# A two-layer recurrent encoder trunk: the residual kept token-major, output projections with x stationary

## The chip, the cores and the metric

The kernel runs on one core of a Trainium2 chip. A core has five engines that run on their own: TensorE (PE in the profile, with its weight loads as PEld), VectorE (DVE), ScalarE (ACT), GpSimd (POOL) and SyncE (SP), which here only starts transfers. They meet through semaphores. The metric is the device time of one execution in microseconds; lower is better.

## The reference

The input x is 256 tokens by 2048 features, float32. Two layers follow each other; each is a mixer and a gated MLP, each behind an RMSNorm and added to the residual:

```
for layer in range(2):
    hn = rmsnorm(h, norm_mix_g[layer])
    h = h + (mlstm_mixer if layer == 0 else hgrn_mixer)(hn, ...)
    h = h + conv_glu(rmsnorm(h, norm_ffn_g[layer]), ...)
return rmsnorm(h, final_g)
```

`rmsnorm` divides by the root of the mean square over the 2048 features of a token and multiplies by a gain per feature. The mLSTM mixer projects hn to q, k, v, an output gate and 32 gate columns, runs a bidirectional matrix memory over 8 heads, and projects 2048 features back (`w_out`). The HGRN mixer does the like with 16 heads. `conv_glu` projects to 2 x 5504 features, runs a centred convolution of width 3 over the tokens on one half, and projects `gelu(c) * v` back to 2048 (`w_down`).

## The kernel before

Every large product is an exact-enough float32 product made of three fast ones. A weight piece of 1024 columns is fetched as `raw` (SyncE's queue, 1 MB a transfer), rounded on ScalarE to `wh` (L145), and the remainder `wl` is left by a subtraction on VectorE (L146). Activations are held in the same way: a tile `xt` has the rounded value in its first 256 columns and the remainder in the next 256. The product is `wh*xh + wl*xh + wh*xl`.

`stream` walks over a list of chunks, each with a weight source, `nk` inner tiles of 128, and a function `done` that takes the sums out of PSUM. Weight pieces are made three ahead (`LOOK`), with three raw buffers and four of `wh` and `wl`. A chunk has one of these forms:

- "fm", feature-major: the weights are stationary. Two blocks of 128 output features are made; for each inner tile and block, one matmul streams the 512 columns of `xt` (hi and lo at once) and one streams 256 columns against `wl` (L196, L197). The output has features on partitions and tokens along the row.
- "tm", token-major: x is stationary. 512 output features are made for two halves of 128 tokens; for each inner tile and half, three matmuls of 512 columns stream `wh`, `wl`, `wh` (L186 to L188). The output has tokens on partitions.

Queries, keys, decays and the whole up projection are "fm"; values and output gates are "tm". The four kinds of output projection (mLSTM, HGRN, and the two parts of each feed-forward stage, which splits its 43 hidden tiles into 22 and 21) are "fm" chunks of 256 features, eight for each (`project`, L298).

The residual `hx` is feature-major: 16 blocks `hT[k]` of 128 features by 256 tokens. When a projection chunk is done, ScalarE copies the upper half of the sums (`b`, L309) and VectorE adds both halves to the block (L310, L311). `Norm.add` then makes the next stage's `xt` by `split` (L203 on ScalarE, L204 on VectorE) with the gain in it, and GpSimd squares the block and adds it to a running sum (L245, L247). After the last block two matmuls with ones sum the squares over the partitions (L253); `finish` takes the power on GpSimd (L279), spreads the result over the partitions by a diagonal and two matmuls (L285), and copies it out as `R` (L287). Since the factor is per token, `R` is applied to the results of the next stage, not to its inputs.

The last norm's blocks are scaled by their gain into `hg` (L232). The very last chunk is made block by block with 256-column matmuls (L175); at its end the squares are closed, and eight tiles of 512 columns are multiplied by the factor, six on VectorE and two on GpSimd (L787), and stored by eight transfers from two queues (L788).

The recurrences of the heads run beside the projections. They are generators, kept in `Side` and moved on by a count of time that each inner tile adds to (`tick`); `until` and `drain` force them. The program order that comes out is then put through a scheduler that may move instructions within an engine; the hardware runs each engine's list in order.

Of the kernel before, what the change touches and what calls it, by code (L numbers as in the profile page):

```python
# [15 lines left out]
P = 128  # L16
T = 256
# [13 lines left out]
    ("mix_g", 2 * KT), ("ffn_g", 2 * KT), ("a_head_g", KT), ("b_head_g", KT), ("final_g", KT),  # L31
# [21 lines left out]
def trunk_kernel(ctx, tc, xT, pp_d, cst_d, w_first, w_aq, w_ak, w_av, w_ao, w_aout,  # L53
                 w_bq, w_bv, w_bg, w_bout, w_up, w_down, out, mscr, stop=9):
# [15 lines left out]
    hT = [hx[:, k] for k in range(KT)]  # L70
    ident = cst[:, C_ID:C_ID + P]
# [46 lines left out]
    def split_weights(chunks):  # L118

        first = True  # L120
        for ch in chunks:
            total = ch.nk * ch.width
            cuts = [0]
            if ch.last and total % 1024:
                cuts.append(total % 1024)
# [24 lines left out]
    def stream(chunks):  # L150
# [10 lines left out]
        for ch in chunks:  # L161
# [4 lines left out]
            while k < ch.nk:  # L166
                fetch()
                wh, wl, n = ready.pop(0)
                if ch.last:
                    for f in range(2):  # L170
                        for kk in range(n):
                            x, c = ch.x(k + kk), kk * 256 + f * P
                            terms = ((wh, 0), (wl, 0), (wh, T))
                            for i, (w, o) in enumerate(terms):
                                pe.matmul(ps[f][:, 0:T], w[:, c:c + P], x[:, o:o + T], start=(k + kk == 0 and i == 0),  # L175
                                          stop=(k + kk == ch.nk - 1 and i == 2))
                    k += n
                    continue
# [43 lines left out]
    class Norm:  # L222
        def __init__(self, gname, goff, final=False, first=False):
            self.first = first
            self.g, self.o, self.final = gname, goff, final
            self.xs, self.pc = [], None

        def add(self, k):
            if self.final:
                if k % 2 == 0:  # L230
                    self.xs.append(keep.tile([P, 2, T], F32, tag=f"xt{k}", name=f"hg{k}"))
                act.activation(self.xs[k // 2][:, k % 2], hT[k], AF.Copy, scale=col(self.g, self.o + k))  # L232
            else:
                t = keep.tile([P, 2 * T], F32R, tag=f"xt{k}", name=f"xt{k}")
                split(t, hT[k], col(self.g, self.o + k))
                self.xs.append(t)
            if self.first:
                return
# [10 lines left out]
            if k >= (KT - 3 if self.final else KT - 1):  # L249
                if self.pc is None:  # L250
                    self.pc = [aux("pc") for _ in range(2)]
# [621 lines left out]
```

## Time and profile before

| | |
|---|---|
| median of the runs | 2469.77 us (2469.3 to 2469.8, 3 runs) |
| the profiled execution | 2469.78 us, its span 2468.0 us |
| TensorE busy | 2450.2 us, 99% |
| VectorE, ScalarE, GpSimd busy | 1781.9, 1200.8, 272.8 us |
| granted TensorE clock | 0.998 |
| DMA | 449.07 MB, 182 GB/s on average |
| first output projection's first and last matmul | 310.6 and 399.9 us |
| second mixer's output projection | 1646.4 to 1737.1 us |

In rows of groups, the numbers behind the bar are the busy time in us and the mean of one instruction in ns, then the idle time of that engine just before them and what ended it. Matmuls are pipelined: their durations overlap, so the sum of a group's durations is more than the time it takes. The distance between starts in the timeline is what a matmul costs the stream. Rows of the timeline give start (us), duration (us), engine, line, operation and tiles. Rows of stretches give the stretch, its length, then each engine's busy time, then granted clock, DMA share and GB/s. Rows of the chain give start, duration, engine, tile, line.

### The profile page before, as it was taken

To read this page: it belongs to the slowest core of one execution; us is meant where nothing else is said; L and a number is where in the kernel's file an instruction comes from. 1 tells how busy PE (TensorE), PEld (TensorE's weight loads), DVE (VectorE), ACT (ScalarE), POOL (GpSimd) and SP (SyncE) were. 2 spreads that over 40 slices of the span, in tenths; PEclk is the share of its full clock that TensorE was granted. 3 is DMA by queue.
4 is the path that set the end of the run, shared out by engine and by line. 5 is a ranking of instruction groups with operands and counts; after the bars stand their busy time and mean duration, and the time that the engine had idled before them with its cause. 6 is when DMAs were issued, how large, how long until landed. Compare 5 with 4: busy or idle time off the path is not lost.

```text
span 2468.0 us, 35972 instructions
## 1 busy us (share of the span) xinstructions
PE 2450.2 (99%) x13950; PEld 2134.1 (86%) x13950; DVE 1781.9 (72%) x2975; ACT 1200.8 (49%) x1810; POOL 272.8 (11%) x341
## 2 busy tenths in 40 slices
PE   9999999999999999999999999999999999999998
PEld 7888888888888888888888888888888888888887
DVE  7766577777656777678888888887777755677754
ACT  6655455444444445444444444445544444444443
POOL 0100032000000000132222222224000000000022
PEclk9999999999999999999999999999999999999999
DMA  7654555666556555555454544446555555666553
GB/s 260 189 178 167 177 183 188 190 189 191 186 189 199 188 188 189 180 194 178 157 168 154 164 161 156 163 145 202 187 189 188 188 188 190 192 192 193 183 190 124
DMA packets 65915, 449.07 MB, mean 182 GB/s; under 512 B 7616, under 2 KB 8128, under 8 KB 15568
## 3 DMA queue, kind: packets, MB, share of 16 engines
q1 hardware_dynamic: 63936, 443.29, 55.4%
q0 software_dynamic: 800, 2.16, 0.6%
q8 instruction: 109, 1.79, 0.3%
q10 hardware_dynamic: 1008, 1.32, 0.1%
q14 instruction: 62, 0.51, 0.1%
HBM read 444.58 MB, written 2.16 MB: 181 GB/s over the span
## 4 chain that ended last, share of the span: by engine, by line
PE 90%; DVE 7%; issue 1%; ACT 1%; DMA 0%; DVEq 0%; POOL 0%; POOLq 0%
PE mm L196 50%; PE mm L197 25%; PE mm L187 3%; PE mm L188 3%; PE mm L186 3%; DVE wl L146 3%; DVE QK L627 1%; PE pd L626 1%; DVE km L609 1%; PE pn L439 1%; PE mm L175 1%; DVE AT L604 1%; PE py L651 1%; DVE qm L609 1%; DVE G L586 0%
## 5 line engine op out<-in xcount | busy, mean ns | idle before, releaser
L146 DVE TENSOR_TENSOR wl<-raw,wh 128x1024 fp32r<-128x1024 f32 (+1 forms) x864 | 1047.1, 1213 | 553.6 <-ACT wh L145 540.6
L145 ACT CAST wh<-raw 128x1024 fp32r<-128x1024 f32 (+1 forms) x864 | 884.4, 1024 | 895.8 <-PE mm L196 500.4
L196 PE MATMUL mm<-xt,wh 128*128 128x512 f32 x3776 | 1318.5, 395 | 0.0
L197 PE MATMUL mm<-xt,wl 128*128 128x256 f32 x3776 | 1050.8, 278 | 0.0
L196 PEld LDWEIGHTS mm<-xt,wh 128*128 128x128 f32 x3776 | 708.0, 188 | 161.2
L197 PEld LDWEIGHTS mm<-xt,wl 128*128 128x128 f32 x3776 | 709.9, 188 | 0.9
L196 PE MATMUL mm<-g,wh 128*128 128x512 f32 x1334 | 462.6, 394 | 0.0
L197 PE MATMUL mm<-g,wl 128*128 128x256 f32 x1334 | 369.5, 277 | 0.0
L196 PEld LDWEIGHTS mm<-g,wh 128*128 128x128 f32 x1334 | 250.1, 188 | 58.1
L197 PEld LDWEIGHTS mm<-g,wl 128*128 128x128 f32 x1334 | 250.4, 188 | 0.0
L186 PE MATMUL mm<-wh,xt 128*128 128x512 f32 x512 | 203.9, 402 | 2.2 <-ACT xt L203 2.2
L187 PE MATMUL mm<-wl,xt 128*128 128x512 f32 x512 | 204.5, 399 | 0.4 <-DVE wl L146 0.4
L188 PE MATMUL mm<-wh,xt 128*128 128x512 f32 x512 | 201.9, 396 | 0.0
L208 ACT COPY b<-mm 128x256 f32<-128x256 f32 x237 | 87.7, 370 | 178.9 <-PE mm L197 178.9
L242 POOL TENSOR_TENSOR acc<-hx 128x256 f32<-128x256 f32 x4 | 4.8, 1205 | 1239.7 <-DVE hx L311 1239.7
L186 PEld LDWEIGHTS mm<-wh,xt 128*128 128x128 f32 x512 | 96.1, 189 | 21.0 <-ACT xt L203 2.5
L187 PEld LDWEIGHTS mm<-wl,xt 128*128 128x128 f32 x512 | 97.0, 189 | 18.4 <-DVE wl L146 0.8
L188 PEld LDWEIGHTS mm<-wh,xt 128*128 128x128 f32 x512 | 97.0, 189 | 18.4
L196 PE MATMUL mm<-yb,wh 128*128 128x512 f32 x256 | 89.6, 396 | 0.0
L196 PE MATMUL mm<-ya,wh 128*128 128x512 f32 x256 | 89.1, 394 | 0.0
L245 POOL TENSOR_TENSOR sq<-hx 128x256 f32<-128x256 f32 x52 | 62.1, 1202 | 197.8 <-DVE hx L311 195.6
L209 DVE TENSOR_TENSOR a<-mm,b 128x256 f32<-128x256 f32 x86 | 36.5, 424 | 51.0 <-ACT b L208 50.9
(185 smaller groups left out, 2083.2 us busy)
## 6 DMA issues: line engine op xcount, KB each, us to landing
raw<-in_w_up SPq DMA_DIRECT2D x172, 1024.0 KB, 5.2
raw<-in_w_down SPq DMA_DIRECT2D x64, 1024.0 KB, 4.9
raw<-in_w_bq SPq DMA_DIRECT2D x48, 1024.0 KB, 5.1
raw<-in_w_ao SPq DMA_DIRECT2D x16, 1024.0 KB, 4.9
raw<-in_w_aout SPq DMA_DIRECT2D x16, 1024.0 KB, 5.2
raw<-in_w_bv SPq DMA_DIRECT2D x16, 1024.0 KB, 4.9
raw<-in_w_bg SPq DMA_DIRECT2D x16, 1024.0 KB, 4.9
raw<-in_w_bout SPq DMA_DIRECT2D x16, 1024.0 KB, 5.1
```

Of the source, the lines that this page charges most:

```text
L145: act.copy(wh[:, :m], r)
L146: dve.tensor_tensor(wl[:, :m], r, wh[:, :m].bitcast(F32), ALU.subtract)
L175: pe.matmul(ps[f][:, 0:T], w[:, c:c + P], x[:, o:o + T], start=(k + kk == 0 and i == 0), stop=(k + kk == ch.nk - 1 and i == 2))
L186: pe.matmul(ps[t], xh, wh[:, c], start=st, stop=False)
L187: pe.matmul(ps[t], xh, wl[:, c], start=False, stop=False)
L188: pe.matmul(ps[t], xl, wh[:, c], start=False, stop=sp)
L196: pe.matmul(ps[f], wh[:, c:c + P], x, start=st, stop=False)
L197: pe.matmul(ps[f][:, 0:T], wl[:, c:c + P], x[:, 0:T], start=False, stop=sp)
L208: act.copy(b, ps[:, T:2 * T])
L209: dve.tensor_tensor(dst, ps[:, 0:T], b, ALU.add)
L245: eng.tensor_tensor(s, hT[k], hT[k], ALU.mult)
L609: dve.tensor_copy(m.rearrange("k (m p j) -> k m p j", p=2, j=h), blocks(z, h, 0, T))
```

## The change

The residual is kept token-major: the same memory `hx` is read as `hm`, 2 halves of 128 tokens by 2048 features. It is no longer what the first norm leaves behind; after the first chunk is finished with the transposed input, the token-major x is loaded over it by two transfers on GpSimd's queue.

- Output projections become four "tm" chunks of 512 features instead of eight "fm" chunks of 256. VectorE adds the sums of a token half to the residual in one instruction of 512 columns; the copy `b` and the second add are gone. The weights `w_aout`, `w_bout` and `w_down` are laid out in blocks of 512 columns.
- The sum of squares of a chunk comes from ScalarE: a square with an accumulator, for each half (`square`). GpSimd's squares and sums and the two matmuls with ones are gone, except in the first norm.
- The next stage still wants features on partitions. A side job `turn` transposes the chunk's eight 128x128 blocks on TensorE (into PSUM, two features blocks at a time) and splits from there. The job takes its turn 2.5 counts after the chunk, and asking for a missing tile or for `R` forces it.
- The last norm has its own class. Its gain is loaded spread over the partitions. Chunks are multiplied by the gain on VectorE as they come. In the last chunk, once the remaining weight pieces are all made, the first token half is finished over all of them, then the second; each half is closed by itself: add, square, a partial sum made earlier, power on GpSimd, four scalings of 512 columns (two on VectorE, two on ScalarE) and four transfers.
- The output leaves token-major, and the host no longer transposes it.

The diff, cut to its core:

```diff
+    hm = hx.rearrange("p k t -> p (k t)").rearrange("p (a c) -> p a c", a=2)
...
-                if ch.last:
-                    for f in range(2):
-                        for kk in range(n):
-                            x, c = ch.x(k + kk), kk * 256 + f * P
-                            terms = ((wh, 0), (wl, 0), (wh, T))
-                            for i, (w, o) in enumerate(terms):
-                                pe.matmul(ps[f][:, 0:T], w[:, c:c + P], x[:, o:o + T], ...)
+                if ch.last and k + sum(p[2] for p in ready) + n == ch.nk:
+                    pieces_, k0 = [(wh, wl, n)] + ready, k
+                    for t in range(2):
+                        k = k0
+                        for wh, wl, n in pieces_:
+                            for kk in range(n):
...
+                                pe.matmul(ps[t], xh, wh[:, c], start=False, stop=False)
+                                pe.matmul(ps[t], xh, wl[:, c], start=False, stop=False)
+                                pe.matmul(ps[t], xl, wh[:, c], start=False, stop=k == ch.nk - 1)
+                                k += 1
+                        ch.half(ps[t], t)
+                    return
...
+        def take(self, k, src):
+            self.xs[k] = keep.tile([P, 2 * T], F32R, tag=f"xt{k}", name=f"xt{k}")
+            split(self.xs[k], src, col(self.g, self.o + k))
...
+        def add(self, c):
+            if c == 0:
+                self.ss = ev.tile([P, 2, 4], F32, tag="ss8", bufs=2, name="ss8")
+            cs = slice(512 * c, 512 * c + 512)
             for t in range(2):
+                square(hm[:, t, cs], self.ss[:, t, c:c + 1])
+            side.push(self.turn(c))
+
+        def turn(self, c):
+            yield 2.5
+            for k0 in (4 * c, 4 * c + 2):
+                pz = aux("pz")
+                for k in (k0, k0 + 1):
+                    for t in range(2):
+                        o = (k - k0) * T + t * P
+                        pe.transpose(pz[:, o:o + P], hm[:, t, k * P:(k + 1) * P], ident)
+                for k in (k0, k0 + 1):
+                    self.take(k, pz[:, (k - k0) * T:(k - k0 + 1) * T])
+                yield 1.0
+            if c == 3:
+                ss = self.ss
+                dve.tensor_tensor(ss[:, :, 0:2], ss[:, :, 0:2], ss[:, :, 2:4], ALU.add)
+                dve.tensor_tensor(ss[:, :, 0:1], ss[:, :, 0:1], ss[:, :, 1:2], ALU.add)
+                self.finish([ss[:, t, 0:1] for t in range(2)])
...
+    class FinalNorm:
+        def begin(self, mp):
...
+            pool.dma_start(self.g, fg_d.broadcast_to([P, D]))
...
+        def half(self, ps, t):
+            side.drain()
+            cs = slice(D - 512, D)
+            h = hm[:, t, cs]
+            dve.tensor_tensor(h, h, ps, ALU.add)
+            square(h, self.ss[:, t, 3:4])
+            last = self.mp.tile([P, 512], F32, tag="fl", bufs=2, name="fl")
+            dve.tensor_tensor(last, h, self.g[:, cs], ALU.mult)
+            rc = self.rc[:, t:t + 1]
+            dve.tensor_scalar(rc, self.ss[:, t, 3:4], 1.0 / D, rc, ALU.mult, ALU.add)
+            pool.tensor_tensor(rc, rc, hmx[:, 0:1], ALU.pow)
+            for c in range(4):
+                v = last if c == 3 else hm[:, t, 512 * c:512 * c + 512]
+                if c % 2:
+                    act.activation(v, v, AF.Copy, scale=rc)
+                else:
+                    dve.tensor_scalar(v, v, rc, None, ALU.mult)
+                (nc.scalar if c % 2 else nc.sync).dma_start(out[t, :, 512 * c:512 * c + 512], v)
+
+    def square(src, total):
+        jk = ev.tile([P, 512], F32, tag="jk", bufs=1, name="jk")
+        act.activation(jk, src, AF.Square, accum_out=total)
...
-                for f in range(2):
-                    k = 2 * c + f
...
-                    b = ev.tile([P, T], F32, tag="b", bufs=3, name="b")
-                    act.copy(b, ps[f][:, T:2 * T])
-                    dve.tensor_tensor(hT[k], hT[k], ps[f][:, 0:T], ALU.add)
-                    dve.tensor_tensor(hT[k], hT[k], b, ALU.add)
-                    if norm is not None:
-                        norm.add(k)
+                for t in range(2):
+                    h = hm[:, t, 512 * c:512 * c + 512]
+                    dve.tensor_tensor(h, h, ps[t], ALU.add)
+                if norm is not None:
+                    norm.add(c)
             return f_
...
+        chunks = [Chunk("tm", wsrc(c), nk, x, done(c)) for c in range(4)]
+        if isinstance(norm, FinalNorm):
+            chunks[3].last, chunks[3].half = True, norm.half
+        return chunks
...
             def done_first(ps, done_v=done_v):
                 done_v(ps[0:2])
                 gates(ps[2])
+                for t in range(2):
+                    pool.dma_start(hm[:, t], x_d[t])
```

187 lines of the change are left out of this document (84 added, 103 removed).

## The prediction

> **What bounds the kernel now.** I read the page first: busy shares, then the chain of work that ended last.
>
> ```profile
> span 2468.0 us, 35972 instructions
> PE 2450.2 (99%) x13950; PEld 2134.1 (86%) x13950; DVE 1781.9 (72%) x2975; ACT 1200.8 (49%) x1810; POOL 272.8 (11%) x341
> PE 90%; DVE 7%; issue 1%; ACT 1%; DMA 0%; DVEq 0%; POOL 0%; POOLq 0%
> ```
>
> TensorE is busy from the first weights to the last sum, and nine tenths of the chain are its own matmuls. So an edit counts by what it does to three things: TensorE's stream, TensorE's waits, and the stretch behind the last matmul. VectorE, ScalarE and GpSimd time is free as long as they keep ahead of TensorE. The profiled execution took 2469.78 us, 1.8 us around its span of 2468.0; the median of the runs is 2469.77, so I sum against 2469.8.
>
> The groups by line tell how much of the stream the change rewrites.
>
> ```profile
> L196 PE MATMUL mm<-g,wh 128*128 128x512 f32 x1334 | 462.6, 394 | 0.0
> L196 PE MATMUL mm<-ya,wh 128*128 128x512 f32 x256 | 89.1, 394 | 0.0
> L196 PE MATMUL mm<-yb,wh 128*128 128x512 f32 x256 | 89.6, 396 | 0.0
> L175 PE MATMUL mm<-g,wh 128*128 128x256 f32 x84 | 15.4, 284 | 0.0
> L175 PE MATMUL mm<-g,wl 128*128 128x256 f32 x42 | 11.8, 283 | 0.0
> ```
>
> These are the output projections: 1334 + 256 + 256 = 1846 pairs of matmuls, each a 512-column one (L196) and a 256-column one (L197), and 126 of 256 columns in the very last chunk (L175). Their mean durations overlap (394 ns each is longer than the distance to the next), so they price nothing; distances between starts do. The timeline of TensorE gives those, once in a feature-major down projection, once in a token-major chunk of the mLSTM and once in one of the HGRN.
>
> ```profile
> 700.01 0.39 PE L196 MATMUL mm<-g,wh 128*128 128x512 f32 x1
> ...
> 711.80 0.39 PE L196 MATMUL mm<-g,wh 128*128 128x512 f32 x1
> ```
> ```profile
> 174.59 0.39 PE L187 MATMUL mm<-wl,xt 128*128 128x512 f32 x1
> ...
> 186.39 0.39 PE L188 MATMUL mm<-wh,xt 128*128 128x512 f32 x1
> ```
> ```profile
> 1622.72 0.40 PE L186 MATMUL mm<-wh,xt 128*128 128x512 f32 x1
> ...
> 1627.94 0.39 PE L188 MATMUL mm<-wh,xt 128*128 128x512 f32 x1
> ```
>
> The first two rows are 34 pairs apart: 11.79 / 34 = 346.8 ns a pair, which streams 768 columns. The next two are 52 matmuls apart: 11.80 / 52 = 226.9 ns for 512 columns. The last two are 23 apart: 227.0 ns. Both forms stream the same columns for the same product; 1536 of them take 693.6 ns feature-major and 681 ns token-major.
>
> **The change, part by part.**
>
> *Output projections token-major.* Before: 1846 x 346.8 ns = 640.2 us, and the last chunk's 126 at 9.47 / 79 = 119.9 ns (row below), 15.1 us; together 655.3. After: 118 inner tiles x 4 chunks x 6 = 2832 matmuls of 512 columns; at 227 ns 642.9 us. That is -12.4. Bounds: 226.9 ns gives -12.7; the other end is that the projections gain nothing over the pair's pace, 346.8 x 2 / 3 = 231.2 ns, -0.5. I take 227, since three stages with different neighbours show it.
> The Trainium skill speaks against this term: "TensorE: Matmul & The Clock Gate", section "Back-to-back issue gap", gives a lone warm matmul its columns over 2.4 GHz plus a fixed 2.5 ns, by which only the 986 matmuls saved would count, an estimated -2.5 us. The rows disagree: the pair stands 27 ns over its 768 columns at that clock, the token-major matmul 14 over its 512.
>
> *Transposes.* New: 3 norms x 16 blocks x 2 token halves = 96 transposes of 128x128 on TensorE, in its stream. Before has the same operation at the head outputs, as a group and singly:
>
> ```profile
> 101.45 0.39 PE L186 MATMUL mm<-wh,xt 128*128 128x512 f32 x1
> 101.68 0.60 PE L467 MATMUL pz<-cst,y 128*128 128x128 f32 x4
> 102.03 0.48 PE L187 MATMUL mm<-wl,xt 128*128 128x512 f32 x1
> ```
> ```profile
> 1255.71 0.37 PE L197 MATMUL mm<-xt,wl 128*128 128x256 f32 x1
> 1255.91 0.27 PE L672 MATMUL pz<-cst,y 128*128 128x128 f32 x1
> 1255.94 0.48 PE L196 MATMUL mm<-xt,wh 128*128 128x512 f32 x1
> ```
>
> Four together push the next matmul 0.35 us back, 88 ns each; a single one pushes it by 0.23 - 0.115 = 0.115 us. In the changed program's instruction order, the eight of a chunk stand mostly as 1 + 3 + 4 or 1 + 1 + 6. With 16 singles at 0.115 and 80 at 88 ns: +8.9 us; all grouped +8.4, all single +11.0.
>
> *Sums of squares.* The ones-matmuls over the accumulated squares go for three norms, and the group inside the last chunk. The chain has that group:
>
> ```profile
> 2439.92 9.47 PE mm L175 x79
> 2449.39 0.34 PE pc L253 x4
> 2449.73 5.27 PE mm L175 x43
> ...
> 2455.03 0.43 DVE hx L305
> ...
> 2455.55 0.44 DVE sq L245
> ...
> 2456.03 0.62 PE pc L253 x4
> ...
> 2456.98 0.71 POOL rc L279
> ...
> 2458.05 0.73 PE pr L285 x4
> ...
> 2460.49 2.39 DVE hg L787 x4
> ```
>
> 4 x 0.34 = -1.4 us. GpSimd's squares and sums, VectorE's second add and ScalarE's copy of each block also go; all of it lay under TensorE's stream, so -0. What replaces it (24 squares with accumulation on ScalarE, splits reading PSUM) lies under the same stream; if that cover were gone, the squares would cost 24 x (0.69 + 0.19), 21 us, by the rows below. The chain that makes `R` (two adds, power, diagonal, two matmuls, copy) keeps its length and starts as the first chunk of the next stage does; that chunk needs R only at its end, 16 x 0.69 = 11.1 us on.
>
> *Waits in front of the transposes.* The rows that price them:
>
> ```profile
> L146 DVE TENSOR_TENSOR wl<-raw,wh 128x1024 fp32r<-128x1024 f32 (+1 forms) x864 | 1047.1, 1213 | 553.6 <-ACT wh L145 540.6
> L467 PE MATMUL pz<-cst,y 128*128 128x128 f32 x32 | 4.9, 272 | 0.0
> ```
>
> Each group waits for VectorE's add of that token half into the residual. ScalarE's splits wait behind the transposes and the next weight casts behind these. The first transpose stands some 20 matmuls, 4.6 us, behind the next chunk's first. The adds need 0.03 for the release, up to 1.21 for a weight subtraction just begun (L146), and 2 x 0.69: 2.6 us, or 3.9 where another subtraction stands between the halves. So I take 0. The weight pieces run three ahead of use (3 x 2.7 us), which covers the casts.
>
> *Loading x token-major.* Two transfers of 1 MB on GpSimd's queue, ahead of the first norm's power on that queue and of everything else it issues. They wait for the last readers of the old contents, long done when that power starts; before shows that engine idle there, and the DMA with room:
>
> ```profile
> 37.40 0.70 POOL L279 TENSOR_TENSOR rc<-rc,mhalf 128x2 f32<-128x2 f32 x1 [36.12 <-DVE rc L278]
> 10.00:15.00 5.00, 5.00 (x20) 4.03 (x19) 4.10 (x11) 5.00 (x11) 0.00 (x0) 1.00 1.03 416
> 25.00:30.00 5.00, 5.00 (x25) 4.16 (x24) 4.16 (x7) 2.00 (x4) 0.00 (x0) 1.00 0.87 247
> 30.00:35.00 5.00, 5.00 (x25) 4.14 (x24) 2.42 (x3) 2.32 (x4) 0.00 (x0) 1.00 0.68 210
> ```
>
> Up to 416 GB/s have been moved and about 230 are in use, so 2.1 MB more take some 11 us beside the weights; the first reader of x is the first chunk of the mLSTM's output projection, which starts past 300 us. I take 0; if the weights were late by half of that, about +5. The final gain, spread over the partitions (1 MB, same queue, at the start of the second feed-forward stage), is hidden likewise.
>
> *The end.* Before, from the end of the last matmul (2449.73 + 5.27 = 2455.0) to the end of the span: 13.0 us. After, the second token half alone is left, and the first delays it. In the new order 14 matmuls (3.2 us) of half 1 follow half 0's last. Prices:
>
> ```profile
> L787 DVE TENSOR_TENSOR hg<-hg,pr 128x512 f32<-128x512 f32 x6 | 3.7, 680 | 1.0 <-ACT R L287 1.0
> L689 ACT ACTIVATE sg<-mm,rc 128x512 f32<-128x512 f32 x8 | 5.5, 690 | 5.9 <-PE mm L188 5.9
> L452 ACT ACTIVATION_READ_ACCUMULATOR jk<-y 128x1 f32 x16 | 3.1, 192 | 0.0
> L788 SPq DMA_DIRECT2D out<-hg x4: 344/370/766, 2459.9 to 2462.9; - x4
> DMA to landing us min/median/max: 2.1/2.8/3.8
> ```
>
> Half 0: add 0.7, square 0.7 + 0.2, small step 0.2, power 0.15 + 0.7, two scalings about 1.3, two issues 0.8: VectorE is free some 0.7 us, ScalarE 1.6 us after the last matmul. Half 1 then: add to 1.4, square from 1.6 to 2.5, small step and power to 3.5, two scalings to 4.9, two issues to 5.7, landing 2.1 after the last one's start (5.3 + 2.1 = 7.4), and 1.3 from landing to the end (before: 2468.0 less 2462.9 + 3.8): 8.7 us. That is -4.3; with the landings at their maximum (3.8) -2.6; without half 0 in the way -5.2.
>
> Sum: -12.4 + 8.9 - 1.4 - 4.3 = -9.2; 2469.8 - 9.2 = 2460.6 us. The terms' ends give 2469.8 - 12.7 + 8.4 - 1.4 - 5.2 = 2458.9, and 2469.8 - 0.5 + 11.0 - 1.4 - 2.6 + 5 = 2481.3 with everything against it at once.
>
> **The rivals.** *No better pace* (231.2 ns): what the pair loses, the new form loses otherwise, for instance because the weights are now the moving operand with fresh semaphores. -0.5 in place of -12.4: 2472.5. Against it stand three token-major runs at 227. Whoever goes by the skill's fixed gap comes out 2 us below that.
> *Late adds* (the slower side): at each of the twelve chunk ends TensorE stands before the transposes, because the add of the second half queues behind another weight subtraction. At 1.21 us each 14.5 us: 2475.1. It decides from 9.2 / 12 = 0.77 us a chunk end on. For it: VectorE runs its queue in order, and the subtractions themselves wait for casts. Against it: the 4.6 us above.
> *Transposes at full length*: 96 x 0.272 (the busy mean of L467's 32) = 26.1 us in place of 8.9: 2477.8. The four in 0.35 us speak against it. The skill's same page, section "Part 4: PE-mode transpose", gives about 275 ns in a kernel's context; by the rows that is latency, not distance.
> *The end does not shrink*: the output's landings set it, as before: 2464.9.
>
> **How the numbers follow.** Chances: the forecast 0.65 (own range 2457 to 2465), no better pace 0.08, late adds 0.10, full-length transposes 0.03, an end that does not shrink 0.10, something at the load of x 0.04. The likeliest gives 2460.6. The range 2456.5 to 2471 leaves out late adds, full transposes and half of the pace case. A change under 0.2% (4.9 us) can't be told from none here. Faster: nearly all of the forecast and a third of the end case, 0.64. Same: the pace case for the greater part, the rest of the end case, the forecast's edge and the load, 0.23. Slower: 0.13.
>
> **What would show it.** Token-major output projections with starts 227 ns apart; transposes that push their neighbours by 0.35 us per four, with no idle time of TensorE before them that VectorE's add ended; no idle time between 25 and 60 us; and 8 to 10 us from the last matmul to the end. The prediction is wrong if the add of the residual appears as a releaser of TensorE, if the projections' starts are 230 ns or more apart, or if the HGRN stage, whose matmuls are untouched, lasts otherwise than before.

## The result, and the profile after

The changed kernel takes 2473.83 us (median of 21 runs, 2473.29 to 2474.34), the kernel before in the same session 2469.77 us: 1.0016 times as long, 95% interval 1.0009 to 1.0023. That is 4.1 us slower, within the 0.2% that the prediction called no change, and 2.8 us above the range of 2456.5 to 2471.

The head of the page of the changed kernel: span, busy times, and the chain by engine.

```profile
span 2472.1 us, 33659 instructions
...
PE 2459.1 (99%) x13032; PEld 2102.3 (85%) x13032; DVE 1719.2 (70%) x2816; ACT 1188.3 (48%) x1751; POOL 153.4 (6%) x235
...
PE 93%; DVE 5%; issue 1%; ACT 1%; DMA 0%; SPq 0%; POOLq 0%; POOL 0%; DVEq 0%
```

TensorE runs 918 instructions fewer and is busy 9 us longer. The other three engines got lighter, as intended, and it is worth nothing. So the question is what the same engine does more slowly. The stages tell where. A feed-forward stage runs its first 22 hidden tiles as up A and down A, then the other 21 as up B and down B; up B is called part B below, and up A part A. The times are measured from the first matmul of one stage to the first of the next (us; the last row from the end of the last projection matmul to the end of the span):

| stage | before | after | difference |
|---|---|---|---|
| start to first matmul | 7.1 | 6.65 | -0.45 |
| mLSTM | 303.5 | 303.6 | +0.1 |
| its output projection | 89.7 | 90.8 | +1.1 |
| layer 0: up A, down A | 245.0, 122.0 | 245.5, 120.7 | +0.5, -1.3 |
| layer 0: **up B**, down B | 233.0, 116.5 | 237.4, 117.9 | **+4.5**, +1.4 |
| HGRN | 529.7 | 529.9 | +0.3 |
| its output projection | 91.1 | 92.3 | +1.3 |
| layer 1: up A, down A | 245.0, 122.0 | 245.5, 120.6 | +0.5, -1.5 |
| layer 1: **up B**, down B | 233.0, 117.6 | 237.4, 115.3 | **+4.5**, -2.3 |
| last projection matmul to the end | 13.0 | 8.4 | -4.6 |

The two numbers in bold belong to a stage whose instructions the change does not touch: part B of the up projection, 1344 feature-major matmuls with the same operands. The view by line, for part B (count, shortest/median/longest duration in ns, first and last start), first of the kernel before, then of the changed kernel, there with part A above it:

```profile
L196 PE MATMUL mm<-xt,wh x672: 392/394/395, 767.3 to 999.9; 128*128 128x512 f32 x168
```
```profile
L199 PE MATMUL mm<-xt,wh x681: 390/392/397, 410.4 to 646.2; 128*128 128x512 f32 x171
...
L199 PE MATMUL mm<-xt,wh x672: 393/398/403, 767.2 to 1004.3; 128*128 128x512 f32 x168
```

672 pairs of matmuls have 671 distances: 232.6 / 671 = 346.6 ns a pair before, 237.1 / 671 = 353.4 ns after. Part A of the changed kernel keeps (646.2 - 410.4) / 680 = 346.8. The pair has two paces, some 6.7 ns apart, and both are steady over hundreds of microseconds. Part B of both layers makes +8.95 us. From 770 to 995 us, inside part B, the granted clock is 1.00 in both kernels and TensorE is busy all the time, so neither the clock nor a wait makes the difference. Part A follows token-major matmuls as directly as part B does, and it starts slow too: its first ten pairs take 352 ns each. Behind its transposes the pair takes 346.6.

The second surprise lies in the down projections. The timeline of one token-major chunk of layer 0: its first matmul, the first of inner tile 16 (96 matmuls later), and the first of the next chunk (36 later).

```profile
646.51 0.39 PE L189 MATMUL mm<-wh,g 128*128 128x512 f32 x1
...
668.29 0.40 PE L189 MATMUL mm<-wh,g 128*128 128x512 f32 x1
...
676.69 0.39 PE L189 MATMUL mm<-wh,g 128*128 128x512 f32 x1
```

Tiles 0 to 15 go at 21.78 / 96 = 226.9 ns, as forecast; tiles 16 to 21 at 8.40 / 36 = 233.3 ns. Tiles 0 to 15 lie in the buffers that also serve the head outputs, tiles 16 to 21 in a pool of the stage's own.

The new transposes and the last projection matmul in the timeline of the changed kernel, and the end of its chain:

```profile
406.29 0.28 PE L200 MATMUL mm<-xt,wl 128*128 128x256 f32 x1
406.41 0.60 PE L268 MATMUL pz<-cst,hx 128*128 128x128 f32 x4
406.76 0.47 PE L199 MATMUL mm<-xt,wh 128*128 128x512 f32 x1
407.07 0.28 PE L200 MATMUL mm<-xt,wl 128*128 128x256 f32 x1
...
2463.23 0.40 PE L178 MATMUL mm<-wh,g 128*128 128x512 f32 x1
```
```profile
2460.41 0.70 DVE hx L338
2461.13 0.73 ACT jk L355 x2
2462.19 0.55 POOL frc L344
2462.73 2.81 issue
2465.54 0.60 POOLq L907
2466.17 0.72 ACT hx L348
2466.89 0.61 ACT fl L348
```

Four transposes push the next matmul back by 0.35 us, just as at the head outputs. But that matmul then stands 0.31 us ahead of its successor, where 0.23 is usual, so the group costs 0.43 us in all. The last projection matmul starts at 2463.23 and ends 0.4 later; from there 8.4 us are left.

### The profile page after: what moved, and what is told of

It is laid out like the page before. It is cut to its first block, busy times and chain, and to the rows that moved or that the text cites. A ratio compares the mean times of both kernels' runs of the same rounds, so it can differ in the third digit from the quotient of the medians.

```text
span 2472.1 us, 33659 instructions
## 1 busy us (share of the span) xinstructions
PE 2459.1 (99%) x13032; PEld 2102.3 (85%) x13032; DVE 1719.2 (70%) x2816; ACT 1188.3 (48%) x1751; POOL 153.4 (6%) x235
## 3 DMA queue, kind: packets, MB, share of 16 engines
q10 hardware_dynamic: 1008, 1.32, 0.1%
## 4 chain that ended last, share of the span: by engine, by line
PE 93%; DVE 5%; issue 1%; ACT 1%; DMA 0%; SPq 0%; POOLq 0%; POOL 0%; DVEq 0%
PE mm L199 34%; PE mm L200 17%; PE mm L190 12%; PE mm L191 12%; PE mm L189 12%; DVE wl L145 2%; PE pd L688 2%; DVE QK L689 1%; PE pn L499 1%; DVE km L671 1%; PE py L713 1%; PE pz L268 0%; DVE AT L666 0%; DVE qm L671 0%; ACT wh L144 0%
## 5 line engine op out<-in xcount | busy, mean ns | idle before, releaser
L145 DVE TENSOR_TENSOR wl<-raw,wh 128x1024 fp32r<-128x1024 f32 (+1 forms) x848 | 1030.5, 1216 | 608.9 <-ACT wh L144 600.4
L191 PE MATMUL mm<-wh,g 128*128 128x512 f32 x674 | 263.9, 392 | 0.0
L189 PE MATMUL mm<-wh,g 128*128 128x512 f32 x674 | 263.6, 391 | 0.0
L190 PE MATMUL mm<-wl,g 128*128 128x512 f32 x674 | 263.4, 391 | 0.0
L191 PEld LDWEIGHTS mm<-wh,g 128*128 128x128 f32 x674 | 126.6, 188 | 27.5
L190 PEld LDWEIGHTS mm<-wl,g 128*128 128x128 f32 x674 | 126.6, 188 | 27.2
L189 PEld LDWEIGHTS mm<-wh,g 128*128 128x128 f32 x674 | 126.6, 188 | 27.2
L688 PEld LDWEIGHTS pd<-qm,km 128*128 128x128 f32 x448 | 62.9, 191 | 10.2 <-PE mm L191 4.2
L688 PE MATMUL pd<-qm,km 128*128 128x128 f32 x448 | 66.1, 276 | 1.2 <-DVE qm L671 1.1
```

What stands on the lines that cost most here:

```text
L145: dve.tensor_tensor(wl[:, :m], r, wh[:, :m].bitcast(F32), ALU.subtract)
L189: pe.matmul(ps[t], xh, wh[:, c], start=st, stop=False)
L190: pe.matmul(ps[t], xh, wl[:, c], start=False, stop=False)
L191: pe.matmul(ps[t], xl, wh[:, c], start=False, stop=sp)
L688: pe.matmul(pd[:, c], km[:, c], qm[:, c], start=True, stop=True)
```

## The experiments

Two theories stood against each other for part B. *History*: what ran before it decides the pace, and the changed kernel puts token-major matmuls directly in front of it. *Placement*: the pace belongs to the stage, to where its buffers lie or what runs beside it. For tiles 16 to 21 the question was their place in memory, their position in the chunk, or history. Below, "a stretch" is a row of matmuls of one form with nothing between, and its "phase" is a name for which of the two paces it is in.

### Four transposes ahead of part B

```diff
+    def brk(n):
+        pz = aux("brk")
+        for i in range(n):
+            tc.keep_in_program_order(pe.transpose(pz[:, i * P:(i + 1) * P], ident, ident))
...
-                                    begin if f0 + i == 0 else None))
+                                    begin if f0 + i == 0 else (lambda: brk(4)) if i == 0 else None))
```

> The changed kernel, with four transposes of the identity into a bank that nobody reads, put between the last token-major chunk of the first down projection and the first pair of up-projection part B, in both layers. Nothing else is changed. History theory: a feature-major run that follows a token-major one directly falls into the slow pace (353.3 ns a pair) and keeps it until short matmuls interrupt it; so part B goes back from 237.4 to 233.0 us per layer, about -8.9 us, and the transposes cost 2 x 0.35 = 0.7: 2473.8 - 8.2 = 2465.6 us. Placement theory: part B is slow because the buffers that it uses lie elsewhere; the pace stays at 353.3 and the time is 2474.5.

Measured: 2474.52 us (10 runs, ratio to the kernel before 1.002, 1.0011 to 1.003). Part B, by line:

```profile
L199 PE MATMUL mm<-xt,wh x672: 395/398/476, 767.4 to 1004.5; 128*128 128x512 f32 x168
```

237.1 / 671 = 353.4 ns: nothing gained. The history theory in the form in which I held it, that a few short operations in between break the slow pace, is wrong.

### The kernel before with six token-major matmuls

```diff
+    def tm6(norm):
+        pz = aux("tm6")
+        for i in range(6):
+            tc.keep_in_program_order(pe.matmul(pz, norm.x(i)[:, 0:P], norm.x(15 - i), start=True, stop=True))
...
-                                    begin if f0 + i == 0 else None))
+                                    begin if f0 + i == 0 else (lambda: tm6(norm)) if i == 0 else None))
```

> The kernel before, with six token-major matmuls of 512 columns whose sums nobody reads (a norm's tile stationary, another moving) put ahead of the first pair of up-projection part B, in both layers; no buffer moves. History theory: part B falls into the slow pace, from 346.7 to 353.3 ns a pair, 232.96 to 237.4 us per layer: +8.9, and the twelve matmuls themselves 2.7: 2469.8 + 11.6 = 2481.4 us. Placement theory: only the twelve matmuls, 2472.5 us, with part B at 346.7 ns.

Measured: 2485.64 us (4 runs, ratio 1.0065, 1.0047 to 1.0083). Part B of layer 0, and the down projection behind it:

```profile
L196 PE MATMUL mm<-xt,wh x672: 393/398/403, 768.4 to 1005.4; 128*128 128x512 f32 x168
...
L196 PE MATMUL mm<-g,wh x336: 395/398/403, 1005.8 to 1124.2; 128*128 128x512 f32 x168
```

Six matmuls, 1.4 us of work, made the next 1008 pairs slow: 237.0 / 671 = 353.2 ns in part B and 118.4 / 335 = 353.4 in the down projection, which in this kernel follows without a break. No buffer moved, so placement alone can't be the cause. The time came out 4.2 us above the history theory's, which had left out the two down projections (336 pairs x 6.6 ns = 2.2 us each).

### One or two transposes; a cut first pair; another order of the last matmuls

The first of these kernels is the one with four transposes with `brk(1 + layer)` in place of `brk(4)`. The second:

```diff
+                            if f == 0 and st and ch.cut:
+                                for o in (0, P):
+                                    pe.matmul(ps[f][:, o:o + P], wl[:, c:c + P], x[:, o:o + P], start=False, stop=False)
...
+                            if ch.turned and sp and t == 1:
+                                pe.matmul(ps[t], xl, wh[:, c], start=False, stop=False)
+                                pe.matmul(ps[t], xh, wl[:, c], start=False, stop=sp)
+                                continue
```

> As the run with four transposes in between, but with one in layer 0 and two in layer 1. If any interruption breaks the slow pace, both parts B run at 346.7 ns a pair (some 233 us each). If a group must be long enough to drain something, layer 0 with one stays at 353.3 (237.4 us). By the placement theory both stay at 353.3.

> The changed kernel without added work. Layer 0: the second matmul of the very first pair of part B is cut into two of 128 columns. Layer 1: the last three token-major matmuls before part B come in the order high-high, low-high, high-low of their halves, so that the stationary changes once more just before. Pattern theory (the slow pace is a phase between weight loads and matmuls that any irregular step can shift): at least layer 0 goes to 346.7 ns, 233 us. If only an operation of another kind or a wait breaks it, both stay at 353.3 ns (237.4 us) and the time is 2473.8.

Measured, single runs: 2474.32 and 2473.71 us. Part B lasts 237.5 us in both layers of the first, 237.5 and 237.4 in those of the second. None of the four steps at the border changed the pace.

### A step inside the stretch

```diff
+                            if k == 5 and f == 0 and ch.inner:
+                                ch.inner(1)
                             pe.matmul(ps[f], wh[:, c:c + P], x, start=st, stop=False)
+                            if k == 5 and f == 0 and ch.cut:
+                                for o in (0, P):
+                                    pe.matmul(ps[f][:, o:o + P], wl[:, c:c + P], x[:, o:o + P], start=False, stop=False)
+                            else:
                                 pe.matmul(ps[f][:, 0:T], wl[:, c:c + P], x[:, 0:T], start=False, stop=sp)
```

> The changed kernel with one small step inside part B, after its first 20 matmuls, with no buffer moved: in layer 0 one transpose of the identity that nobody reads, in layer 1 one 256-column matmul cut into two of 128. The run with four transposes ahead of part B left it slow (237.5 us), while in the changed kernel's own rows a transpose after 20 or 22 feature-major matmuls of a slow run is followed by the fast pace. History theory, second form: the slow pace is an alternation that the first pairs after token-major matmuls settle into and that a step inside the run can shift: layer 0 goes from 237.4 to 233.1 us, about -4.4; layer 1 the same if a cut matmul is enough, else 237.4. So 2469.4 us with one layer, 2465.0 with both. Theory that the pace belongs to the stage (what the other engines do, where tiles lie): both stay at 237.4 and the time is 2473.8.

Measured: 2469.52 us (10 runs, ratio 1.0, 0.999 to 1.0009). Part B of layer 0, with a transpose inside, and of layer 1, with one matmul cut in two:

```profile
L201 PE MATMUL mm<-xt,wh x672: 394/398/477, 767.1 to 1004.3; 128*128 128x512 f32 x168
...
L201 PE MATMUL mm<-xt,wh x672: 389/392/446, 2110.8 to 2343.6; 128*128 128x512 f32 x168
```

The transpose did nothing (353.5 ns). The cut took layer 1 to 232.8 / 671 = 346.9 ns, and 4.3 us off the kernel. The same columns, the same operands, one instruction more: the stage and its places are not the cause.

### The same cut where it is not needed

The kernel before with the cut's lines of the last diff, switched on in the first chunk of part B in both layers.

> The kernel before, whose part B runs at the fast pace, with the same cut in the sixth inner tile of its first chunk, both layers. If the cut brings any run to the fast pace, nothing changes: 2469.8 us, part B 233.0. If it shifts a phase by a fixed amount (so that a slow run becomes fast and a fast one may become slow), part B goes to 237.4 us and, since nothing interrupts the run, the down projection behind it to 118.7: 2469.8 + 2 x (4.4 + 2.3) = 2483.2 us.

Measured, a single run: 2483.3 us. Part B of layer 0 and the down projection behind it:

```profile
L196 PE MATMUL mm<-xt,wh x672: 392/398/450, 766.8 to 1003.9; 128*128 128x512 f32 x168
...
L196 PE MATMUL mm<-g,wh x336: 395/398/403, 1004.3 to 1122.7; 128*128 128x512 f32 x168
```

Here the cut made a stretch at 346.6 ns slow: 237.1 / 671 = 353.4. So a cut heals nothing by itself. It moves the stretch from one of two phases into the other, and the phase holds until something shifts it again. The 2483.2 worked out from this picture was met within 0.1.

### The cut wherever a token-major chunk leads straight into a long stretch

```diff
+            n0 = len(chunks)
...
+            chunks[n0].cut = part == 1
...
             chunks.append(Chunk("fm", w_aq[pr], KT, norm.x, done_q))
+            chunks[-1].cut = pr > 0
```

> The changed kernel with one 256-column matmul cut into two of 128, in the sixth inner tile, in both first chunks of part B and in the three query chunks of the mLSTM that follow a token-major chunk. History theory, as the run with a cut in layer 1 alone bears it out (233.1 us in place of 237.4): both parts B at 233.1 us, -8.7, and the query and key chunks of three head pairs at 346.7 ns a pair from the cut on, 3 x 55 pairs x 6.6 ns = -1.1: 2473.8 - 9.8 = 2464.0 us, faster than the kernel before by 0.2%. If the pace in the mLSTM has another cause than in part B, its 1.1 stays out: 2465.1. If the cut's effect in layer 1 came from the stage and not from the cut, layer 0 stays at 237.4: 2469.5.

Measured: 2464.59 us (11 runs), 0.9981 of the kernel before (0.9972 to 0.999). Part B took 233.1 us in both layers (346.9 ns a pair, -8.6 us), the mLSTM 302.8 instead of 303.6. The stage as a whole lasts 303.1 to 305.0 us in kernels that do not touch it, so its length decides nothing, but its pairs do. The second query and key stretch, without its first pairs:

```profile
L199 PE MATMUL mm<-xt,wh x57: 391/391/445, 188.7 to 208.2; 128*128 128x512 f32 x57
```

The median is 391 ns, where the changed kernel has 398. In each of the three stretches the pairs behind the cut stand 346.7 ns apart, and each stretch is 0.25 us shorter than in the changed kernel: 0.75 us of the forecast 1.1. This settles where the first loss lies: with the phase shifted back, what was missing returns, and the change then is faster than the kernel before.

### Tiles 16 to 21: position or place

Three kernels: inner tiles exchanged between the two pools; the raw weights' buffers placed behind `wh` and `wl`; and the buffers of tiles 0 to 15 placed behind the weights.

```diff
-                g = slot(i, "g", mp)
+                g = slot(i - 6 if i >= 6 else KT + i, "g", mp)
```
```diff
-                raw = wpool.tile([P, 2048], F32, tag="raw", bufs=RAW, name="raw")
+                raw = rpool.tile([P, 2048], F32, tag="raw", bufs=RAW, name="raw")
```
```diff
-        where = keep if j < KT else more
+        where = ypool if j < KT else more
```

> The changed kernel with the places of the inner feed-forward tiles exchanged: tiles 0 to 5 lie in the stage's own pool, 6 to 21 in the buffers that served 0 to 15. Place theory for the slower token-major matmuls (233 ns for tiles 16 to 21 against 226.7): tiles 0 to 5 are at 233 ns, 6 to 21 at 226.7. Position theory (late tiles are slow, whatever their place): 16 to 21 at 233 ns still. History theory (a slow pace once entered stays): all at 233 ns, some 2.5 us more per down projection. Time by place or position about 2473.8 us.

> The changed kernel with the buffers of the raw weights placed behind those of the two weight halves, which so lie 24 KB lower in each partition; the inner tiles 16 to 21 stay where they were. If the slower 233 ns of tiles 16 to 21 come from sharing a part of the memory with the weight halves, they go to 226.7 ns or move to other tiles (about -3.5 us: 2470.3, or no change in the sum); if they come from their own place alone, they stay at 233 ns and the time is 2473.8.

> The changed kernel with the sixteen buffers of the head outputs and of inner tiles 0 to 15 placed behind the weights: at 140 to 173 KB of each partition in place of 75 to 108 KB; the weights lie 33 KB lower; tiles 16 to 21 stay at 180 to 192 KB. Upper-memory theory for the slower token-major matmuls: the tiles moved become slow as well (233 ns in place of 226.7), in both output projections and in the first sixteen inner tiles of four down projections: 2304 matmuls x 6.6 ns = +15.2 us: 2489.0. If the border lies above 173 KB, or if the slowness belongs to the stage pool itself (for instance to its neighbours a, v and c being written), nothing changes: 2473.8.

Measured: 2473.92, 2474.02 and 2483.24 us, single runs. The first chunk of layer 0's down projection with the tiles exchanged (its first matmul, the first of tile 6, the next chunk's first), and with tiles 0 to 15 moved up (first, first of tile 16, next chunk's first):

```profile
646.22 0.39 PE L189 MATMUL mm<-wh,g 128*128 128x512 f32 x1
...
654.62 0.40 PE L189 MATMUL mm<-wh,g 128*128 128x512 f32 x1
...
676.41 0.40 PE L189 MATMUL mm<-wh,g 128*128 128x512 f32 x1
```
```profile
648.76 0.39 PE L190 MATMUL mm<-wh,g 128*128 128x512 f32 x1
...
671.15 0.39 PE L190 MATMUL mm<-wh,g 128*128 128x512 f32 x1
...
679.55 0.39 PE L190 MATMUL mm<-wh,g 128*128 128x512 f32 x1
```

Exchanged, the first six tiles take 8.40 / 36 = 233.3 ns and the others 21.79 / 96 = 227.0: it is the place. With the raw buffers moved, nothing changed (233.3 still). Moved up, tiles 0 to 15 take 22.39 / 96 = 233.2. That fitted "upper memory", but the kernel came out 5.8 us below the 2489.0 of that theory. The rows of its two parts B tell why for the most part:

```profile
L200 PE MATMUL mm<-xt,wh x672: 392/395/397, 772.0 to 1004.6; 128*128 128x512 f32 x168
...
L200 PE MATMUL mm<-xt,wh x672: 393/398/403, 2118.0 to 2355.0; 128*128 128x512 f32 x168
```

Layer 0's part B follows token-major matmuls directly and yet is fast, 232.6 / 671 = 346.6 ns. So not every such border gives the slow phase: how the matmuls ahead were spaced counts too. Part B of layer 0 gave 4.5 us back. Most of the remaining 1.3 is the price of the tiles: the six projections became 14.0 us longer, where 2304 matmuls at 6.6 ns had been put at 15.2.

### The same tiles at other offsets

A gap ahead of the stage pool moves tiles 16 to 21; in one of the kernels a gap of 320 bytes ahead of the weights moves these too. The gaps of the four kernels in bytes for layers 0 and 1: 1728 and 16384; 192 and 128 (with the weights moved); 704 and 128; 320 and 320.

```diff
             box["mp"] = stack.enter_context(tc.tile_pool(name="ff", bufs=1))
+            box["mp"].tile([P, (1728, 16384)[layer] // 4], F32, name="gap")
```

> The changed kernel with an unused tile ahead of the others in the stage pool of the feed-forward blocks: 1728 bytes a partition in layer 0, so that tiles 16 to 21 lie at the same offset within 2048 bytes as the fast tiles 0 to 15; 16384 bytes in layer 1, higher but at an unchanged offset. Alignment theory: layer 0's tiles 16 to 21 go from 233.3 to 226.7 ns, -1.7 us (264 matmuls in two down projections' parts), layer 1 stays: 2472.1. Upper-memory theory: all stay at about 233 ns, 2473.8.

> The changed kernel with the weight buffers 320 bytes higher, so that the weight halves and tiles 16 to 21 both lie at offset 384 within 512 bytes, while the other stationary tiles stay at 64. Relative theory (the moving weights and the stationary tile must lie alike): tiles 16 to 21 go to 226.7 ns, and those at 64 may become slow. Absolute theory (the stationary tile's own offset): tiles 16 to 21 stay at 233.3 ns, all others at 226.7.

> The changed kernel with tiles 16 to 21 at offset 64 within 1024 bytes in layer 0 (704 bytes of gap) and at 64 within 512 but 576 within 1024 in layer 1 (128 bytes of gap). If the offset counts within 512 bytes, both layers' tiles go to 226.7 ns, -3.6 us: 2470.2. Within 1024: layer 0 alone, 2472. Within 2048 alone: neither, 2473.8.

> The changed kernel with tiles 16 to 21 at offset 192 within 512 bytes in layer 0 and 256 in layer 1. Known so far: 64 and 128 fast (226.7 to 226.9 ns), 384 slow (233.3), 448 mostly slow (232.6). A border between 128 and 384 is expected; the two values say on which side of it 192 and 256 lie. Time between 2470.2 (both fast) and 2473.8 (both slow).

Measured, single runs: 2473.41, 2487.18, 2470.26 and 2472.55 us. The first is 1.3 us above the alignment theory's 2472.1 because the mLSTM, which it does not touch, lasted 305.0 us in place of 303.6; the two down projections of layer 0 lost 1.9, as that theory had it (1.7). Rows of the first chunk of a down projection, each time its first matmul, the first of tile 16 and the next chunk's first. Layer 0 with the gap of 1728 bytes:

```profile
647.97 0.39 PE L189 MATMUL mm<-wh,g 128*128 128x512 f32 x1
...
669.76 0.39 PE L189 MATMUL mm<-wh,g 128*128 128x512 f32 x1
...
677.92 0.39 PE L189 MATMUL mm<-wh,g 128*128 128x512 f32 x1
```

With the weights moved to 384, layer 0:

```profile
652.90 0.39 PE L190 MATMUL mm<-wh,g 128*128 128x512 f32 x1
...
674.88 0.40 PE L190 MATMUL mm<-wh,g 128*128 128x512 f32 x1
...
683.06 0.39 PE L190 MATMUL mm<-wh,g 128*128 128x512 f32 x1
```

With tiles at 192 in layer 0, then at 256 in layer 1 (here only tile 16's first and the next chunk's first):

```profile
668.44 0.40 PE L189 MATMUL mm<-wh,g 128*128 128x512 f32 x1
...
676.80 0.39 PE L189 MATMUL mm<-wh,g 128*128 128x512 f32 x1
...
2011.88 0.39 PE L189 MATMUL mm<-wh,g 128*128 128x512 f32 x1
...
2020.12 0.39 PE L189 MATMUL mm<-wh,g 128*128 128x512 f32 x1
```

At 1088 within 2048, which is 64 within 512, the tiles take 8.16 / 36 = 226.7 ns, higher in memory than before; so it is not the upper memory. Layer 1's, 16 KB higher at their old offset, stay at 232.5. In the third kernel both layers are cured (226.7 ns), and its 2470.26 us is what counting within 512 bytes foretold. Both its parts B still last 237.4 us, so it was not the slow tiles ahead that made part B slow. With the weights at 384, the tiles that lie at 384 as well need 8.18 / 36 = 227.2, and those at 64, fast until now, 21.98 / 96 = 229.0: the distance between the stationary tile and the moving weights counts, not the tile's own offset. All readings by that distance (stationary tile less moving weights, within 512 bytes; offsets from the memory plan of each kernel):

| distance | ns a matmul | read in |
|---|---|---|
| 0 | 226.7 to 227.2 | tiles 0 to 15; every cured case; tiles at 384 with the weights at 384 |
| 128 | 232.2 | tiles at 192, weights at 64 |
| 192 | 228.9, 229.0 | tiles at 256, weights at 64; tiles at 64, weights at 384 |
| 320 | 233.3 | layer 0 of the changed kernel; exchanged tiles; tiles moved up |
| 384 | 232.5 | layer 1 of the changed kernel |

The two cases at 192 agree although no address of theirs does. The border that the last expectation asked for does not exist as such: the order is not by size of the distance.

The kernel with moved weights shows the price of a wrong distance for the rest. It is 13.4 us slower than the changed kernel, mostly in feature-major stretches that were fast; part A of layer 0 now needs (652.5 - 412.3) / 680 = 353.2 ns:

```profile
L200 PE MATMUL mm<-xt,wh x681: 388/397/398, 412.3 to 652.5; 128*128 128x512 f32 x171
```

Behind 400 us this kernel has no feature-major stretch at the fast pace: of the windows of twelve pairs with nothing between, counted end to end, none is fast and 252 are slow, against 133 and 119 in the changed kernel. In the pair the weights are the stationary operand, here at distance 320 from `xt`. So it looks as if at this distance the pair had the slow pace alone; whether a cut could shift it was not tried. Not every distance does that to the pair: in the down projection of the kernel before, tiles 16 to 21 were the moving operand, 256 bytes from the stationary weights, and their pairs took 346.7 ns like the others.

### Both cures

The kernel with the cuts, with gaps of 1728 and 1664 bytes, so that tiles 16 to 21 lie at distance 0 in both layers.

> The run with the cut in both parts B and the query chunks, and besides tiles 16 to 21 moved in both layers to the offset (1088 within 2048 bytes) at which layer 0's went to 226.7 ns. Both causes add: 2464.6 less 2 x 1.9 (down A 120.7 to 119.7, down B 117.9 to 117.0 as in the run that moved layer 0) = 2460.8 us. If the pace of the last tiles sets the phase in which part B starts, the cut may turn a part B that was fast into a slow one: +4.4 a layer, up to 2469.6.

Measured: 2460.72 us (5 runs), 0.9965 of the kernel before (0.9951 to 0.9978). Part B of layer 0 and of layer 1:

```profile
L199 PE MATMUL mm<-xt,wh x672: 389/391/445, 765.4 to 998.1; 128*128 128x512 f32 x168
...
L199 PE MATMUL mm<-xt,wh x672: 389/391/445, 2102.7 to 2335.5; 128*128 128x512 f32 x168
```

This is the version that beats both kernels, by 8.7 and 13.1 us. The two causes add up: 2473.8 less 9.2 for the cuts leaves 2464.6, and the places took another 3.9; alone, in the kernel with gaps of 704 and 128 bytes, they had taken 3.6.

## Why the prediction was wrong

It summed -12.4 (projections) + 8.9 (transposes) - 1.4 (squares) - 4.3 (end) = -9.2; measured is +4.1. Point by point:

- **The step that failed: everything outside the edited lines counted at zero.** The prediction said that an edit counts by what it does to "TensorE's stream", and priced only the instructions that come, go or move; the 1344 feature-major matmuls of each part B had no term. They cost +8.95 us, two thirds of the miss of 13.3; what the runs showed in the place of an unchanged stage is a pair with two paces, 346.7 and 353.3 ns, of which the edit left part B in the slower. The trace of before showed the effect. In the mLSTM a query chunk follows a token-major chunk directly, and the line's view of it there reads

```profile
L196 PE MATMUL mm<-xt,wh x64: 389/398/403, 113.3 to 135.5; 128*128 128x512 f32 x64
```

  with 22.2 / 63 = 352 ns a pair and a median duration of 398, where part B has 394. I took the pair's price from one place, the down projection, and did not ask whether the same pair had the same pace everywhere, and what preceded it where it had not.
- **Projections, mis-sized.** Forecast 642.9 us for 2832 matmuls at 227 ns. The distances from each start to the next sum to 649.1. Tiles 16 to 21 make 528 matmuls x 6.2 ns = 3.3 of the 6.2; nearly all of the rest lies in 34 matmuls that follow directly on a transpose or on an operation of the heads and stand some 0.32 us ahead of their successor. The others keep to 227 ns. The condition "if the projections' starts are 230 ns or more apart" was met by one fifth of them. (The form before measured 656.3 us against 655.3 in the prediction, so the difference is -7.2; without the 2.2 us of it that belong to the new transposes it is -9.4, in place of -12.4.)
- **Transposes, mis-sized.** The forecast read their price off the start of the next matmul. By that measure the 96 cost 8.4 us, forecast 8.9. But the matmul behind a group hands on more delay: in the kernel before, the one at 102.03 us, which the forecast's rows show, is followed at 102.35, 0.32 later. With this the 96 cost 11.0 us, 115 ns each, the top of the forecast's bounds. The rival of full lengths (26.1) falls all the same.
- **The end, right in sum.** 8.4 us against 8.7, from 13.0 before. The order of the steps in the chain is that of the forecast: add, square, power, two scalings. Two sizes were off and nearly cancel: the last transfer is issued 3.9 us after the last matmul's end instead of 5.3, and the end follows 4.5 us later instead of 3.4. The rival that the end would not shrink falls.
- **Waits and the load of x, right.** No add of the residual ends a wait of TensorE: the view of waits names only `xt` (1.8 us, one time), the start's `ones` (1.1), `qm` in the HGRN (1.1 in five) and `wl` (0.4). The rival of late adds falls. The first matmul starts 0.45 us earlier than before and the mLSTM lasts as long.
- **HGRN, right in time, by luck.** 529.9 us against 529.7. Its uninterrupted pairs, untouched by the change, take 349.6 ns on average in place of 347.4, some 1.5 us over 660 pairs, and the waits for `qm` fell from 2.7 to 1.1 us. The prediction had meant this stage to show whether untouched matmuls change; they did, and a second difference hid it.
- **No better pace**, the rival at 2472.5, is near the measured time by accident: four fifths of the projections run at the forecast 227 ns, and what was lost was lost elsewhere. The fixed gap of a lone matmul that the Trainium skill gives ("TensorE: Matmul & The Clock Gate", section "Back-to-back issue gap") is one pace for one form; in the streams here the runs show two.

The measured terms are -9.4 (projections), +11.0 (transposes), -1.45 (the sixteen matmuls with ones of before, from start to start), -4.6 (end), +8.95 (part B) and -0.45 (the earlier first matmul); they sum to the +4.1. With both cures the kernel stands at 2460.72 us where 2460.6 was forecast. That it is so close is partly luck: 0.75 us of it comes from the mLSTM's cuts, which cure what was slow before the change too, and against that stand the transposes, 2.1 us dearer than forecast. What the forecast lacked most was a reason to expect the untouched matmuls to keep their pace.

## What to carry to other kernels

On a stream of matmuls that is never idle, an edit can change the pace of instructions that it does not touch, by 2% here, so price a form at several places of the trace of before and ask what stood ahead of each. Compare stages whose instructions are the same first when a time comes out wrong; the difference of medians (394 against 398 ns in one row) shows it at a glance. Where the stationary and the moving tile are both planned by hand, keep their offsets alike within 512 bytes (five distances were read here, and 0 was the fastest); and where a long stretch is slow, splitting one matmul in it is a cheap trial, to be judged by the trace, since the same cut did harm where the stretch was fast.

## What the runs showed of the hardware that was not expected

- One pair of matmuls (512 and 256 columns, with other weights each) has two steady paces, 346.7 and 353.3 ns. A stretch keeps the one it fell into over up to 237 us and on into the next stage (118 us), until something shifts it. Cutting one 256-column matmul into two of 128, at some 0.1 us, shifted it in all seven parts B that had the cut inside, five times to the fast and twice to the slow side, and in the three stretches of the mLSTM to the fast side; in the very first pair it did not. A transpose inside the stretch did not, nor did one, two or four ahead of it.
- The 512-column matmul with another stationary tile each time takes 226.7 to 233.3 ns by the distance of the stationary tile from the moving one within 512 bytes of a partition's memory, with nothing else changed. The page "SBUF — State Buffer" of the Trainium skill, section "A bandwidth-pool intuition that's wrong (but worth ruling out)", gives the weight loads a second, independent read port beside the moving operand's; read that way the distance should not matter, and here it does.
- 226.7, 233.3, 346.7 and 353.3 ns are 34, 35, 52 and 53 times 6.67 ns, as if starts were kept to a grid. That is a reading of the numbers; no run tested it.

Open stays what sets the phase at a border. A long stretch directly behind a token-major chunk began slow nearly everywhere. It began fast in the kernel whose projections went at 233 ns, except for part B of layer 1, and in the HGRN of the kernel with tiles at distance 128. Transposes of the HGRN's heads stand at changes of pace in both directions (353.6 to 346.7 ns behind 1261 us in the changed kernel, 346.8 to 353.7 behind 1256 us in the kernel before), while the one tried inside part B changed nothing. Why a distance of 192 bytes costs less than one of 128 isn't known either.
